# Hybrid decoder block: narrow split weights two to a buffer, the first weights of three projections asked for ahead, a last unit in halves

## The chip, the cores and the metric

The kernel runs on one core of a Trainium2 chip. The metric is device time in microseconds (us); lower is better. The engines are named as the profile names them: PE (matmuls) with PEld (its weight loads), DVE (vector), ACT (scalar), POOL (GpSimd) and SP, whose queue issues the transfers.

## The reference, cut to what matters

One decoder layer over 2048 positions of width 1024 in fp32. The change touches the feed-forward part and the last norm; what comes before them is the same in both kernels.

```python
def rmsnorm(x, g):
    y = x * lax.rsqrt(jnp.mean(x * x, axis=-1, keepdims=True) + NORM_EPS)
    return y * g
...
    x = x + mixed                       # mixers and output projection, unchanged here
    h2 = rmsnorm(x, norm2_g[l])
    ffn = (jax.nn.silu(h2 @ w_ffn_gate[l]) * (h2 @ w_ffn_up[l])) @ w_ffn_down[l]
    x = x + ffn
return rmsnorm(x, norm_f_g)
```

`D_MODEL` is 1024, `D_FF` 2816.

## The kernel before

Activations are kept transposed: 128 channels by 512 positions is a tile. The sequence is worked in two halves, and each half in two columns `j` of 512 positions. Every large product is a Strassen-like **unit** (`unit`, L385): a 2x2 block of weights times a 2x2 block of activations in seven products (`PRODUCTS`) instead of eight. An fp32 number is split into a high and a low part in fp32r (`split`, L151: ACT writes the high part at L153, DVE the low part at L154), and each product step is three matmuls, high x high, high x low, low x high (L381, L382, L383).

**Weights.** `raw_weights` loads four blocks of a unit into a tile `raw` (two buffers). `unit_weights` forms the sums of blocks on POOL (L364, L365, L366, L371) and splits seven quarters. Each quarter takes a tile `wq` of [128, 2, 512] from a pool of four buffers, whatever its width: 512 columns in the up projections, 384 in the later units of the down projection, 256 in its first four units (`wdown_first`).

**Feed-forward.** For each half, `ffn_up` runs 22 units over the operands `ops` (28 tiles of 512 KB, high and low parts); its results are split and stored to DRAM (`so`, then `sa`). `ffn_down` runs four groups of row blocks; group 0 has two blocks and four narrow units, the others three blocks and four units of 384 columns. In the first half the operands of `ffn_up` are made on the way; for the second half they lie in DRAM (`shB`, `shT`), and `load_h2` loads all 28 while `ffn_down(0)` ends. Each such load is placed after the load of the second-to-last weights (`raw_loads[-2]`).

**The last unit** (`last_unit`, L1019) multiplies without Strassen: four products of 18 matmuls over 512 positions, for two row blocks and two columns. To each belong a residual add (DVE, L1060), a square (ACT, L1062) and a gain (ACT, L1029). `norm(j)` sums the squares over partitions with a matrix of ones (PE, L1034 and L1035, fp32), takes Ln and Exp (ACT, L199, L200) and a Newton step (DVE, L201, L163 to L165), and copies the factor from PSUM to SBUF for POOL (ACT, L1037). `scale(j)` multiplies the eight tiles of a column by it, six on DVE and two on POOL (L1043), and stores each (SP, L148).

**Order.** A scheduler places the instructions on each engine from its own estimates, with the data dependences and some given orders (`tc.issue_after`). Each engine and SP's queue then works strictly in that order. The background work (splitting and storing the up projection's results, the next norm) is mixed in by `tick`.

Of the kernel before, what the change touches and what calls it, by code (L numbers as in the profile page):

```python
# [11 lines left out]
F32R = mybir.dt.float32r  # L12
U32 = mybir.dt.uint32
AF = mybir.ActivationFunctionType
ALU = mybir.AluOpType
# [36 lines left out]
def tile_hymba_block(ctx, tc, x, xt, win, wa, wgu, wout, wffn, wdown, wdown_first, small, out):  # L52
# [94 lines left out]
    def store(dst, src):  # L147
        return nc.sync.dma_start(dst, src)  # L148
# [92 lines left out]
    def no_operands():  # L241
        return {b: [] for _, b in PRODUCTS}
# [87 lines left out]
    def plain_unit(src, ops):  # L330
# [11 lines left out]
                us.append((r, j, settled(o, True), False))  # L342
        return us

    def weight_quarter(src):
        n = src.shape[-1]
        h = wqp.tile([P, 2, PB], F32R, name="wq", tag="wq")[:, :, 0:n]
        split(src, h[:, 0, :], h[:, 1, :])
        return h

    def raw_weights(src):
        n = src.shape[-1]
        raw = rawp.tile([P, 4 * PB], F32, name="raw", tag="raw")[:, 0 : 4 * n]
        raw = raw.rearrange("p (a n) -> p a n", a=4)
        raw_loads.append(load(raw, src))
        return raw

    def unit_weights(src):
        raw = raw_weights(src)
# [6 lines left out]
        pool.tensor_tensor(a11, s1, a11, ALU.subtract)  # L366
# [4 lines left out]
        pool.tensor_tensor(a12, a12, a11, ALU.subtract)  # L371
        w["S4"] = weight_quarter(a12)
        w["A22"] = weight_quarter(a22)
        return w

    def product_step(o, w, op, k, first):
        n = len(op)
        c = slice(k * P, (k + 1) * P)
        wh, wl = w[:, 0, c], w[:, 1, c]
        xh, xl = op[k][:, 0, :], op[k][:, 1, :]  # L380
        pe.matmul(o[:], wh, xh, start=first and k == 0, stop=False, skip_group_check=True)  # L381
        pe.matmul(o[:], wh, xl, start=False, stop=False, skip_group_check=True)  # L382
        return pe.matmul(o[:], wl, xh, start=False, stop=k == n - 1, skip_group_check=True)  # L383

    def unit(src, ops, into=None, onto=None):  # L385


        w = unit_weights(src)

        def mul(i, o=None):  # L390
            first = o is None
            o = bank() if first else o
            n, m = PRODUCTS[i]
            for k in range(len(ops[m])):
                product_step(o, w[n], ops[m], k, first)
            tick()
            return o

        def copied(name, o, at):
            if onto is not None:  # L400
                return plus(onto[at], o)
            t = tt(name) if into is None else into[at]
            act.activation(t[:], o[:], AF.Copy)  # L403
            return t

        def plus(t, o):
            dve.tensor_tensor(t[:], o[:], t[:], ALU.add)  # L407
# [499 lines left out]
    def ffn_up(half, ops):  # L907
        for m in range(NF // 2):
            us = unit(wffn[2 * m], ops)
# [12 lines left out]
            background.insert(0, split_later(s_act[half][m], values))  # L922
# [17 lines left out]
    def ffn_down(half):  # L940

        y, early = {}, {}

        def group_op(m, n):
            return early.pop((m, n)) if (m, n) in early else act_op(half, m, n)

        for u, m0 in enumerate(GROUPS):
# [10 lines left out]
            for d0 in range(0, KD, 2):  # L958
# [6 lines left out]
                if u == 0:  # L965
                    for d in (d0, d0 + 1):
                        if d < KD - 1:
                            pair = opp.tile([P, 2, PB], F32, name="y", tag="op")
                        for j in range(2):
                            y[d, j] = pair[:, j, :] if d < KD - 1 else bt("y")[:]  # L970
                    unit(src, ops, {(r, j): y[d0 + r, j] for r in range(2) for j in range(2)})
                    continue
                xs = []
                if u < 3:
# [44 lines left out]
    def last_unit(src, ops, b12, y, ssq):  # L1019


        raw = raw_weights(src)
        w = [weight_quarter(raw[:, i, :]) for i in (0, 1, 3, 2)]
        columns = (ops["B11"], ops["B21"]), (b12, ops["B22"])
        with tc.issue_after(last_hi[0].ins):
            act.preload_act_table_set("natural_log_exp_and_others")

        def gain(d, j):
            act.activation(y[d, j], y[d, j], AF.Copy, scale=col(C_GF + d))  # L1029

        def norm(j, q):

            tot, rb = bank("tot"), bank("rb")
            pe.matmul(tot[:], ones[:], ssq[j][:], start=True, stop=False)  # L1034
            pe.matmul(tot[:], ones[:], q[:], start=False, stop=True)  # L1035
            finish_rstd(ssq[j], tot, D, rb)
            act.activation(ssq[j][:], rb[:], AF.Copy)  # L1037
            return rb

        def scale(j, rb):  # L1040
            for d in range(KD):
                eng, by = (pool, ssq[j]) if d in (2, 5) else (dve, rb)
                eng.tensor_tensor(y[d, j], y[d, j], by[:], ALU.mult)  # L1043
                store(out[2 + j, :, d, :], y[d, j])

        for d in range(KD - 2):
            for j in range(2):
                gain(d, j)
        q, rbs = {}, []
        for j in range(2):  # L1050
            for r in range(2):
                o = bank()
                with ExitStack() as stack:
                    if j or r:
                        stack.enter_context(tc.issue_after(done.ins))
                    for i in range(2):
                        for k in range(len(b12)):
                            done = product_step(o, w[2 * r + i], columns[j][i], k, i == 0)
                yy = y[KD - 2 + r, j]
                dve.tensor_tensor(yy, o[:], yy, ALU.add)  # L1060
                q[j] = tt("q")
                act.activation(q[j][:], yy, AF.Square)  # L1062
                gain(KD - 2 + r, j)
                if not r:
                    pool.tensor_tensor(ssq[j][:], ssq[j][:], q[j][:], ALU.add)
                if j and not r:
                    rbs.append(norm(0, q[0]))
        rbs.append(norm(1, q[1]))
        for j in range(2):
            scale(j, rbs[j])  # L1070


    act.preload_act_table_set("natural_log_exp_and_others")
# [136 lines left out]
```

## Time and profile before

| | us |
|---|---|
| runs shown, median of 3 (lowest to highest) | 2093.23 (2089.54 to 2095.66) |
| profiled execution, device time | 2092.78 |
| its span, first to last instruction | 2090.8 |
| mean granted clock of PE in it | 0.993 |

The profiled execution lies 0.45 us under the median of the runs, and 2 us of its time lie outside the span. Where the profile gives a busy time, matmuls overlap: in the steady stretches about 22 of the 128x512 matmuls start in 5 us, though one is shown as 390 ns long. A lost stretch is best seen as matmuls missing from a window.

### The profile page before, as it was taken

Reading aid. Unit: us, or ns where it says so; the run is one execution under the profiler, and the core shown is the slowest. Engines: PE = TensorE matmul, PEld = TensorE weight load, DVE = VectorE, ACT = ScalarE, POOL = GpSimd, SP = SyncE. Lnnn points to the kernel's source line nnn. Section 1 sums busy time; section 2 is a strip of 40 time slices with the busy share of each in tenths; the row PEclk is TensorE's granted clock in tenths of the full one; section 3 lists DMA queues with packets and bytes.
Section 4 is the critical chain, followed back from the end, with each engine's and each line's share of the span. In section 5 each row is a group of like instructions: output and inputs, shape, how many; then the busy total and the mean of one; then the engine's idle time right before and its main releaser. Section 6 shows DMA issues by size and latency. Waiting matters only on the chain.

```text
span 2090.8 us, 26872 instructions
## 1 busy us (share of the span) xinstructions
PE 2029.0 (97%) x9133; PEld 1648.4 (79%) x9133; DVE 1434.0 (69%) x2049; ACT 970.1 (46%) x1921; POOL 876.7 (42%) x637
## 2 busy tenths in 40 slices
PE   5999999999999999999999999999999999999996
PEld 4778888887888887778788878887888888878884
DVE  6669786549754696787887566654776767666665
ACT  5555455656543345454555442223455444453234
POOL 3427222122102464555555434533655544434543
PEclk9999999999999999999999999999999999999998
DMA  7349485424586882654654587698454465488672
GB/s 275 126 152 307 154 338 162 146 96 145 181 306 212 329 286 93 230 224 174 227 222 171 214 326 280 235 358 349 146 206 158 169 228 191 164 349 307 267 272 111
DMA packets 189241, 464.43 MB, mean 222 GB/s; under 512 B 19824, under 2 KB 65072, under 8 KB 179504
## 3 DMA queue, kind: packets, MB, share of 16 engines
q1 hardware_dynamic: 189104, 462.72, 61.3%
q8 instruction: 72, 1.18, 0.2%
q14 instruction: 65, 0.53, 0.1%
HBM read 297.49 MB, written 165.15 MB: 221 GB/s over the span
## 4 chain that ended last, share of the span: by engine, by line
PE 77%; DVE 10%; DMA 6%; issue 3%; ACT 2%; POOL 2%; SPq 1%; DVEq 0%; ACTq 0%; POOLq 0%
PE mm L381 22%; PE mm L383 22%; PE mm L382 22%; DVE wq L154 2%; DVE h L510 2%; PE mm L814 2%; PE mm L815 2%; PE mm L817 2%; DMA op<-shT 1%; DVE so L154 1%; DVE op L154 1%; PE a_ps L578 1%; DMA shT<-so 1%; SPq L145 1%; PE o_ps L738 1%
## 5 line engine op out<-in xcount | busy, mean ns | idle before, releaser
L381 PE MATMUL mm<-op,wq 128*128 128x512 f32 x2499 | 979.6, 394 | 11.0 <-ACT wq L153 4.2
L382 PE MATMUL mm<-op,wq 128*128 128x512 f32 x2499 | 974.5, 390 | 0.0
L383 PE MATMUL mm<-op,wq 128*128 128x512 f32 x2499 | 962.4, 391 | 11.7 <-DVE wq L154 11.2
L154 DVE TENSOR_TENSOR wq<-raw,wq 128x512 fp32r<-128x512 f32 (+2 forms) x626 | 506.7, 815 | 243.2 <-ACT wq L153 241.4
L153 ACT ACTIVATE wq<-raw 128x512 fp32r<-128x512 f32 (+2 forms) x626 | 365.0, 588 | 600.5 <-PE mm L383 461.9
L381 PEld LDWEIGHTS mm<-op,wq 128*128 128x128 f32 x2499 | 469.9, 188 | 123.4 <-ACT wq L153 10.3
L383 PEld LDWEIGHTS mm<-op,wq 128*128 128x128 f32 x2499 | 469.8, 188 | 119.8 <-DVE wq L154 21.5
L382 PEld LDWEIGHTS mm<-op,wq 128*128 128x128 f32 x2499 | 470.1, 188 | 96.5 <-issue 1.0
L366 POOL TENSOR_TENSOR raw<-s,raw 128x512 f32<-128x512 f32 (+2 forms) x97 | 126.5, 1304 | 468.2 <-DVE wq L154 446.9
L364 POOL TENSOR_TENSOR s<-raw 128x512 f32<-128x512 f32 (+2 forms) x97 | 127.2, 1311 | 219.5 <-DMA raw<-in_wffn_dram 95.1
L407 DVE TENSOR_TENSOR y<-mm,y 128x512 f32<-128x512 f32 x185 | 127.4, 689 | 123.3 <-PE mm L383 122.6
L371 POOL TENSOR_TENSOR raw<-raw 128x512 f32<-128x512 f32 (+2 forms) x97 | 125.4, 1292 | 166.0 <-DVE wq L154 158.8
L407 DVE TENSOR_TENSOR c<-mm,c 128x512 f32<-128x512 f32 x198 | 135.6, 685 | 64.6 <-PE mm L383 63.3
L796 POOL TENSOR_TENSOR ssx<-ssx,q 128x512 f32<-128x512 f32 x52 | 76.2, 1479 | 160.7 <-ACT q L795 160.5
L365 POOL TENSOR_TENSOR raw<-raw 128x512 f32<-128x512 f32 (+2 forms) x97 | 136.5, 1407 | 4.9
L403 ACT ACTIVATE c<-mm 128x512 f32<-128x512 f32 x198 | 114.8, 586 | 16.2 <-PE mm L383 14.8
L154 DVE TENSOR_TENSOR so<-t,so 128x512 fp32r<-128x512 f32 x100 | 90.9, 914 | 27.3 <-ACT so L153 26.7
L153 ACT ACTIVATE wq<-s 128x512 fp32r<-128x512 f32 (+2 forms) x97 | 56.8, 585 | 96.2 <-PE mm L383 92.7
L814 PE MATMUL mm<-op,wq 128*128 128x512 f32 x256 | 100.9, 395 | 0.0
L815 PE MATMUL mm<-op,wq 128*128 128x512 f32 x256 | 99.8, 390 | 0.0
L154 DVE TENSOR_TENSOR wq<-s,wq 128x512 fp32r<-128x512 f32 (+2 forms) x97 | 79.7, 822 | 4.1 <-ACT wq L153 3.5
L153 ACT ACTIVATE so<-t 128x512 fp32r<-128x512 f32 x100 | 62.4, 626 | 42.1 <-DMA sa_B<-so 17.8
(178 smaller groups left out, 1849.8 us busy)
## 6 DMA issues: line engine op xcount, KB each, us to landing
raw<-in_wffn_dram SPq DMA_DIRECT2D x44, 1024.0 KB, 5.7
sa_T<-so SPq DMA_DIRECT2D x88, 512.0 KB, 4.9
op<-sa_T SPq DMA_DIRECT2D x88, 512.0 KB, 8.9
sa_B<-so SPq DMA_DIRECT2D x69, 512.0 KB, 3.5
op<-sa_B SPq DMA_DIRECT2D x69, 512.0 KB, 9.2
raw<-in_win_dram SPq DMA_DIRECT2D x23, 1024.0 KB, 5.6
raw<-in_wdown_dram SPq DMA_DIRECT2D x24, 768.0 KB, 5.9
sx<-y SPq DMA_DIRECT2D x48, 256.0 KB, 3.2
```

What stands on the lines that cost most here:

```text
L153: last_hi[:] = [act.activation(hi, src, AF.Copy)]
L154: return dve.tensor_tensor(lo, src, hi.bitcast(F32), ALU.subtract)
L364: pool.tensor_tensor(s1, a21, a22, ALU.add)
L365: pool.tensor_tensor(a21, a11, a21, ALU.subtract)
L366: pool.tensor_tensor(a11, s1, a11, ALU.subtract)
L371: pool.tensor_tensor(a12, a12, a11, ALU.subtract)
L381: pe.matmul(o[:], wh, xh, start=first and k == 0, stop=False, skip_group_check=True)
L382: pe.matmul(o[:], wh, xl, start=False, stop=False, skip_group_check=True)
L383: return pe.matmul(o[:], wl, xh, start=False, stop=k == n - 1, skip_group_check=True)
L407: dve.tensor_tensor(t[:], o[:], t[:], ALU.add)
L814: pe.matmul(o[e, j][:], wh, m[:, 0, :], start=k == 0, stop=False)
L815: pe.matmul(o[e, j][:], wh, m[:, 1, :], start=False, stop=False)
```

## The change

Line numbers of the new kernel are other ones: the matmuls L381 to L383 become L391 to L393, the adds of L407 L417, the copies of L403 L413, the residuals of the last unit L1067.

1. A quarter of at most 256 columns takes half of a `wq` buffer, so that two quarters share one. Units have seven quarters, so a pair can reach over two units.
2. `raw_weights` is called ahead of the operand loads for the first unit of `ffn_down(0)`, `ffn_up(1)` and `ffn_down(1)`. The loads of `load_h2` are placed after the last raw load (`raw_loads[-1]`), which is now the first one of `ffn_up(1)`.
3. In `last_unit` column 1 is worked in two halves of 256 positions, the order of PE and DVE is given by hand, the mean comes from a matrix of 1/1024 (so that the step L201 goes), the Newton step and the gain are folded into DVE's last multiplication, and POOL scales seven of the eight tiles of column 0 and two half tiles of column 1.

```diff
+    beside = []
+
     def weight_quarter(src):
         n = src.shape[-1]
-        h = wqp.tile([P, 2, PB], F32R, name="wq", tag="wq")[:, :, 0:n]
+        if n > PB // 2:
+            beside.clear()
+            h = wqp.tile([P, 2, PB], F32R, name="wq", tag="wq")[:, :, 0:n]
+        elif beside:
+            h = beside.pop()
+        else:
+            both = wqp.tile([P, 2, PB], F32R, name="wq", tag="wq")
+            beside.append(both[:, :, PB // 2 : PB // 2 + n])
+            h = both[:, :, 0:n]
         split(src, h[:, 0, :], h[:, 1, :])
...
     def load_h2():
-        ops, loads = no_operands(), raw_loads[-2]
+        ops, loads = no_operands(), raw_loads[-1]
...
     def ffn_down(half):
         y, early = {}, {}
+        raw = raw_weights(wdown_first[0])
...
-    for half in range(2):
-        ffn_up(half, load_h2() if half else h2)
-        ffn_down(half)
+    ffn_up(0, h2)
+    ffn_down(0)
+    raw = raw_weights(wffn[0])
+    ffn_up(1, load_h2(), raw)
+    ffn_down(1)
```

The last unit, new code only:

```python
known = bt("known", (P, P + KD))
means, gains = known[:, 0:P], known[:, P : P + KD]
dve.memset(means, 1.0 / D)
dve.tensor_scalar(gains, sml[:, C_GF : C_GF + KD], -0.5, None, ALU.mult)
...
def factor(j, tot, s, l, y0):
    rb = bank("rb")
    # three on DVE, in the given order: l = y0 * y0
    # l = (tot + EPS) * l ; rb = (l - 3) * y0
...
def scale(ds, j, s, rb):
    # on DVE: y = (y * gain) * rb, then a store of this part
...
def scale_beside(ds, j, s):
    # on POOL: y = y * ssq[j], then a store of this part
...
o = product(0, 0, whole)
q = residual(o, 0, 0, whole)
...
o = product(1, 0, whole)
q7 = residual(o, 1, 0, whole)
o = product(0, 1, sa)
p = residual(o, 0, 1, sa)
summed(tot[0], ssq[0], whole, first=True)
o = bank()
for n, _ in enumerate(steps(o, 1, 1, sa)):
    if n == 2:
        summed(tot[0], q7, whole, last=True)
l0 = logs(0, tot[0], whole)
p7 = residual(o, 1, 1, sa)
o = product(0, 1, sb)
summed(tot[1], ssq[1], sa, first=True)
rb0 = factor(0, tot[0], whole, *l0)
act.activation(ssq[0][:], rb0[:], AF.Copy)
scale_beside(range(KD - 1), 0, whole)
scale((KD - 1,), 0, whole, rb0)
r = residual(o, 0, 1, sb)
o = bank()
for n, _ in enumerate(steps(o, 1, 1, sb)):
    if n == 0:
        summed(tot[1], p7, sa, last=True)
l1 = logs(1, tot[1], sa)
summed(tot[2], ssq[1], sb, first=True)
summed(tot[2], r, sb)
rb1 = factor(1, tot[1], sa, *l1)
r7 = residual(o, 1, 1, sb)
scale((0, 1), 1, sa, rb1)
summed(tot[2], r7, sb, last=True)
l2 = logs(1, tot[2], sb)
scale((2, 3, 4, 5, 6, 7), 1, sa, rb1)
rb2 = factor(1, tot[2], sb, *l2)
act.activation(ssq[1][:, sb], rb2[:, sb], AF.Copy)
scale_beside((0, 1), 1, sb)
scale((2, 3, 4, 5, 6, 7), 1, sb, rb2)
```

On the engines the change moves instructions in three places. The first is ACT in `ffn_down(0)` between its second and third narrow unit. `wq` are the high parts of quarters, `y` copies of a finished product, `so` the background splits; `raw_11028` (before) and `raw_11021` (now) are the third unit's raw weights. Before:

```order
L403 ACTIVATE y_10928<-mm_10958 128x512
L153 ACTIVATE so_10984<-t2_10785 128x512
L403 ACTIVATE y_10929<-mm_10958 128x512
L153 ACTIVATE so_11003<-t3_10786 128x512
L153 ACTIVATE wq_11031<-raw_11028 128x256
L153 ACTIVATE wq_11037<-s1_11030 128x256
```

Now:

```order
L413 ACTIVATE y_10925<-mm_10951 128x512
L153 ACTIVATE wq_11024<-raw_11021 128x256
L153 ACTIVATE wq_11032<-raw_11021 128x256
L153 ACTIVATE wq_11024<-s1_11023 128x256
L413 ACTIVATE y_10926<-mm_10951 128x512
L153 ACTIVATE so_10977<-t2_10785 128x512
```

The third unit's first quarters have moved ahead of the copy `y` that waits for the second unit's last product. `ffn_down(1)` has the same move.

The second place is SP's queue ahead of `ffn_up(1)`. `shB11` are the first four operand tiles, `sx` and `y` belong to the norm of the first half. Before:

```order
L145 DMA op_12579<-shB11_0_412 128x1024
L148 DMA sx0_1_169<-y_10821 128x512
L148 DMA sx1_3_179<-y_10929 128x512
L148 DMA sx1_2_178<-y_10928 128x512
L148 DMA sx0_3_171<-y_10929 128x512
L145 DMA op_12581<-shB11_1_413 128x1024
L145 DMA y_12738<-sx0_1_169 128x512
L145 DMA y_12830<-sx0_2_170 128x512
L145 DMA op_12583<-shB11_2_414 128x1024
L145 DMA op_12585<-shB11_3_415 128x1024
L145 DMA y_12890<-sx0_3_171 128x512
L148 DMA sx0_4_172<-y_11026 128x512
```

Now:

```order
L145 DMA y_12876<-sx0_3_171 128x512
L148 DMA sx0_4_172<-y_11019 128x512
L145 DMA raw_12565<-in_wffn_dram 128x2048
L145 DMA op_12567<-shB11_0_412 128x1024
L145 DMA op_12569<-shB11_1_413 128x1024
L145 DMA op_12571<-shB11_2_414 128x1024
L145 DMA op_12573<-shB11_3_415 128x1024
L148 DMA sx1_4_180<-y_11019 128x512
L145 DMA op_12575<-shT1_0_416 128x1024
```

The raw load of `ffn_up(1)` stands behind the same store `sx0_4` as before (there it follows the last row shown); it is the four operand loads that have moved, from ahead of it to behind it. The first raw load of `ffn_down` has not moved in SP's queue: it has the same place in both programs, in both halves.

The third place is DVE at the end of the program. `rb` is a norm's factor in PSUM, `known` holds the gains. Before, the last rows:

```order
L1060 TENSOR_TENSOR y<-mm,y 128x512
L201 TENSOR_SCALAR ssx_17376<-tot 128x512
L163 TENSOR_TENSOR l<-y_17857 128x512
L164 SCALAR_TENSOR_TENSOR l<-l,ssx_17376 128x512
L165 SCALAR_TENSOR_TENSOR rb<-l,y_17857 128x512
L1043 TENSOR_TENSOR y<-y,rb 128x512 x6
```

Now:

```order
L1067 TENSOR_TENSOR y<-mm,y 128x256
L1104 SCALAR_TENSOR_TENSOR y<-y,known,rb 128x256 x8
L1084 TENSOR_TENSOR l<-y_17899 128x256
L1087 SCALAR_TENSOR_TENSOR l<-tot,l 128x256
L1093 SCALAR_TENSOR_TENSOR rb<-l,y_17899 128x256
L1104 SCALAR_TENSOR_TENSOR y<-y,known,rb 128x256 x6
```

The last residual now stands ahead of the multiplications of the half before it, and what follows the last norm is half as wide. PE's rows are the same in both programs up to the end of the last unit's second product.

More of the change, by code (lines that the diff above doesn't have):

```diff
@@ L379, in product_step, with unit @@
         wh, wl = w[:, 0, c], w[:, 1, c]
[L380 to L388, printed above, removed]
+        xh, xl = op[k][:, 0, s], op[k][:, 1, s]
+        pe.matmul(o[:, s], wh, xh, start=first and k == 0, stop=False, skip_group_check=True)
+        pe.matmul(o[:, s], wh, xl, start=False, stop=False, skip_group_check=True)
+        return pe.matmul(o[:, s], wl, xh, start=False, stop=k == n - 1, skip_group_check=True)
+    def unit(src, ops, into=None, raw=None, onto=None):
+        w = unit_weights(src, raw)
         def mul(i, o=None):
@@ L1040, in scale @@
[L1040 to L1044, printed above, removed]
-        for d in range(KD - 2):
[L1047 to L1067, printed above, removed]
@@ L1068, in last_unit, with queued @@
-        rbs.append(norm(1, q[1]))
-        for j in range(2):
-            scale(j, rbs[j])
+        known = bt("known", (P, P + KD))
+        means, gains = known[:, 0:P], known[:, P : P + KD]
+        dve.memset(means, 1.0 / D)
+        dve.tensor_scalar(gains, sml[:, C_GF : C_GF + KD], -0.5, None, ALU.mult)
+        halves = slice(0, PB // 2), slice(PB // 2, PB)
+        whole = slice(0, PB)
+        queues = {}
+        def queued(eng, issue):
+            with ExitStack() as stack:
+                if eng in queues:
+                    stack.enter_context(tc.issue_after(queues[eng].ins))
+                queues[eng] = issue()
@@ new lines, in steps, with product, residual @@
+        def steps(o, r, j, s):
+            for i in range(2):
+                for k in range(len(b12)):
+                    queued(pe, lambda: product_step(o, w[2 * r + i], columns[j][i], k, i == 0, s))
+                    yield
+        def product(r, j, s):
+            o = bank()
+            for _ in steps(o, r, j, s):
+                pass
+            return o
+        def residual(o, r, j, s):
+            yy = y[KD - 2 + r, j][:, s]
+            queued(dve, lambda: dve.tensor_tensor(yy, o[:, s], yy, ALU.add))
+            q = tt("q")
+            act.activation(q[:, s], yy, AF.Square)
+            return q
@@ new lines, in last_unit @@
+        for d in range(KD - 2):
+            act.activation(y[d, 0], y[d, 0], AF.Copy, scale=gains[:, d : d + 1])
+        for d in range(2):
+            yy = y[d, 1][:, halves[1]]
+            act.activation(yy, yy, AF.Copy, scale=gains[:, d : d + 1])
+        sa, sb = halves
+        tot = [bank("tot") for _ in range(3)]
+        o = product(0, 0, whole)
+        q = residual(o, 0, 0, whole)
+        act.activation(y[KD - 2, 0], y[KD - 2, 0], AF.Copy, scale=gains[:, KD - 2 : KD - 1])
+        pool.tensor_tensor(ssq[0][:], ssq[0][:], q[:], ALU.add)
```

55 lines of the change are left out of this document (41 added, 14 removed).

## The prediction

> **What bounds the kernel now.** I read the page first: busy shares, then the chain that ended last.
>
> ```profile
> PE 2029.0 (97%) x9133; PEld 1648.4 (79%) x9133; DVE 1434.0 (69%) x2049; ACT 970.1 (46%) x1921; POOL 876.7 (42%) x637
> PE 77%; DVE 10%; DMA 6%; issue 3%; ACT 2%; POOL 2%; SPq 1%; DVEq 0%; ACTq 0%; POOLq 0%
> ```
>
> PE is busy nearly throughout, and the change takes no product away. It can only win back stretches in which PE starves, and the tail. So next come PE's waits, in windows around the two starts of the down projection (the first is shown, the second lists the same two), the start of the second up projection, and the end:
>
> ```profile
> PE mm L381 <- ACT wq L153: 1.5, 1, 1.5
> PE mm L381 <- DVE y L407: 0.8, 1, 0.8
> ...
> PE mm L381 <- ACT c L403: 1.7, 1, 1.7
> PE mm L381 <- DMA op<-shT: 0.4, 1, 0.4
> ...
> PE tot L1035 <- ACT q L1062: 4.5, 1, 4.5
> ```
>
> These waits are short. Since matmuls overlap, I count matmuls in windows of 5 us (columns: stretch, length, busy time and count on PE, PEld, DVE, ACT, POOL, clock, DMA share, GB/s):
>
> ```profile
> 1200.00:1205.00 5.00, 5.00 (x24) 4.14 (x23) 3.67 (x6) 3.21 (x7) 0.00 (x0) 1.00 1.02 410
> 1230.00:1235.00 5.00, 2.71 (x11) 1.50 (x9) 2.11 (x5) 1.95 (x5) 1.27 (x2) 1.00 0.43 175
> 1870.00:1875.00 5.00, 3.08 (x11) 1.93 (x12) 2.69 (x6) 2.25 (x5) 0.97 (x2) 1.00 0.33 134
> 1455.00:1460.00 5.00, 3.31 (x14) 2.36 (x13) 2.86 (x3) 2.81 (x6) 2.50 (x2) 1.00 0.23 66
> ```
>
> A full window counts 23 or 24. Twelve matmuls are missing at 1230 and at 1870, nine at 1455: 12 x 0.227 = 2.7 us, twice, and 2.0 us. (0.227 us is the pitch of a 128x512 matmul, from the tail's rows below.) These three places and the tail are what the change can touch.
>
> **Starts of the down projection.** The timeline there:
>
> ```profile
> 1206.93 0.42 ACT L153 ACTIVATE wq<-s 128x256 fp32r<-128x256 f32 x1 [1.88 <-PE mm L383]
> 1219.84 0.33 SPq L145 DMA_DIRECT2D raw<-in_wdown_first_dram  x1
> 1231.36 0.50 PE L381 MATMUL mm<-op,wq 128*128 128x512 f32 x1 [0.78 <-DVE y L407]
> 1233.05 0.60 ACT L403 ACTIVATE y<-mm 128x512 f32<-128x512 f32 x1 [4.64 <-PE mm L383]
> 1234.07 0.41 ACT L153 ACTIVATE wq<-raw 128x256 fp32r<-128x256 f32 x1
> 1234.52 0.50 PE L381 MATMUL mm<-op,wq 128*128 128x512 f32 x1 [1.51 <-ACT wq L153]
> ```
>
> ACT's splits wait for PE to free a `wq` buffer (1206.93). The third unit's first quarter, on which PE stops until 1234.52, is split only at 1234.07, because in ACT's order it stands behind the copy of 1233.05, which waits for PE itself. With two quarters to a buffer the splits run ahead: in the new order the quarter stands before that copy, its buffer is free by then, and its raw load stands two stores earlier in SP's queue than the one issued at 1219.84. I expect the 1.51 us to go, with the slow restart behind it and short stalls nearby: 2.4 us of the 2.7 plus what is scattered. The 0.78 us stays: two products add into one bank with the same add on DVE between them. Bounds: 0 each if another wait takes its place, 3.4 if the first stall goes too. Two starts: **-4.8 us** (0 to -6.8).
>
> Nothing comes of loading the first weights ahead at these two places: in the program these loads keep their place in SP's queue. The pairing adds no instruction; a buffer is held longer, until both quarters are used, and twice the room covers that.
>
> **Start of the second up projection.** SP's queue, the DMA share there, and a piece of the chain:
>
> ```profile
> 1401.64 0.85 SPq L145 DMA_DIRECT2D op<-shB  x2
> 1405.50 0.36 SPq L145 DMA_DIRECT2D raw<-in_wffn_dram  x1
> 1444.42 0.32 SPq L145 DMA_DIRECT2D op<-shT  x1
> ...
> 1444.42 10.24 DMA op<-shT
> ...
> 1389.00:1392.00 3.00, 3.00 (x15) 2.49 (x14) 1.88 (x4) 0.53 (x1) 1.52 (x2) 1.00 0.23 87
> 1413.00:1416.00 3.00, 3.00 (x15) 2.49 (x14) 2.95 (x4) 0.53 (x1) 2.51 (x3) 1.00 0.85 298
> 1416.00:1419.00 3.00, 3.00 (x15) 2.49 (x14) 1.18 (x2) 0.53 (x1) 1.12 (x1) 1.00 1.02 409
> 1449.00:1452.00 3.00, 3.00 (x15) 2.44 (x14) 0.40 (x1) 0.63 (x1) 0.67 (x1) 1.00 1.02 425
> ```
>
> From 1416 to 1452 the DMA engines are full: 28 operand tiles of 512 KB and raw weights. The last tile is issued at 1444.42, lands 10.24 us later, at 1454.66, and PE waits for it (the 0.4 us above). This chain runs through transfers, so what is queued ahead of it delays PE. Before, the first four tiles, 2.1 MB, went out ahead of the raw weights, the last two of them at 1401.64. Now all four stand behind the raw load, which stays behind a store that waits for DVE, at 1405.50. Those 2.1 MB at 410 GB/s are 5.1 us of transfer that move into the full stretch. Not all is felt: before, I estimate about 1 MB issued just ahead of 1405.50 as still in flight, and 15% of 3 us are free at 1413. I take half: the last tile lands 2.6 us later, and PE with it. The four tiles themselves are needed only some 28 us before the last one (126 matmuls earlier in PE's order x 0.227), at about 1426, so they are in time. Bounds: 0 and +5.1. **+2.6 us.**
>
> **The last unit.** Tail rows, and the issues of the output:
>
> ```profile
> 2060.76 0.69 DVE L1060 TENSOR_TENSOR y<-mm,y 128x512 f32<-128x512 f32 x1 [2.47 <-PE mm L383]
> 2064.64 1.02 PE L1034 MATMUL tot<-ssx,ones 128*128 128x512 f32 x2
> 2064.83 0.69 DVE L1060 TENSOR_TENSOR y<-mm,y 128x512 f32<-128x512 f32 x1 [3.39 <-PE mm L383]
> 2071.03 3.68 DVE L1043 TENSOR_TENSOR y<-y,rb 128x512 f32<-128x512 f32 x6 [0.66 <-ACT ssx L1037]
> 2071.07 2.49 POOL L1043 TENSOR_TENSOR y<-y,ssx 128x512 f32<-128x512 f32 x2 [3.51 <-ACT ssx L1037]
> 2074.63 0.68 DVE L1060 TENSOR_TENSOR y<-mm,y 128x512 f32<-128x512 f32 x1
> 2078.14 0.69 ACT L199 ACTIVATE l<-tot,eps 128x512 f32<-128x512 f32 x1 [1.41 <-PE tot L1035]
> ...
> L148 SPq DMA_DIRECT2D out_dram<-y x16: 332/406/593, 2071.7 to 2086.9; - x16
> ...
> DMA to landing us min/median/max: 2.0/2.7/3.0
> ```
>
> Before, the last residual (2074.63) stands behind six multiplications of column 0, and the whole second norm follows. A product of 18 matmuls takes 2064.83 - 2060.76 = 4.07 us, 0.227 us each. Prices of what is new, from the nearest rows:
>
> ```profile
> 651.29 0.39 PE L740 MATMUL o_ps<-carry,kq 128*128 128x128 f32 x2
> 651.73 0.39 PE L740 MATMUL o_ps<-carry,kq 128*128 128x128 f32 x2
> L153 ACT ACTIVATE wq<-raw 128x256 fp32r<-128x256 f32 x48 | 19.0, 413 | 25.0 <-PE mm L383 16.6 <-POOL raw L366 5.7 <-POOL raw L371 1.9
> L154 DVE TENSOR_TENSOR wq<-s,wq 128x256 fp32r<-128x256 f32 x8 | 3.6, 445 | 0.0
> L510 DVE SCALAR_TENSOR_TENSOR h<-h,sml,rb x16: 740/1402/1787, 708.2 to 744.4; 128x512 f32<-128x512 f32 x16
> L269 POOL TENSOR_TENSOR t<-h x12: 1296/1675/2495, 142.0 to 1067.1; 128x512 f32<-128x512 f32 x12
> ```
>
> No fp32r matmul of 256 columns is in the trace. Four narrow fp32 ones with their weight loads start in 0.44 us, 0.11 each; the wide one takes 0.227. I take 0.12, since half the columns of the wide one is 0.114 and the weight load fits into 0.11. [...]
>
> Now from 2060.76, where both programs stand alike. First half product 2.2, sum matmul 0.85, half of the next product 1.1, second sum 1.0: sums ready at 2065.9. Ln and Exp 0.69 + 0.64, three DVE steps of 0.72, the copy 0.6: POOL starts column 0 at 2070.0. Its seven tiles at 1.25 end at 2078.8, then two halves at some 0.75 at 2080.3. DVE meanwhile does the first half's norm (1.3), the last residual, eight half multiplications (8 x 0.39), the last norm's three steps and six more, and ends near 2079.7, before POOL. In SP's order five stores follow POOL's last one: 5 x 0.41, last issue at 2082.0. Before, from the last issue (2086.9) to the span's end (2090.8) were 3.9 us behind a full queue; with 3.4 now, the end is at 2085.4: -5.4.
>
> Against that: DVE's norm steps with both inputs in SBUF now run beside POOL. The rows of L510 show such a meeting, 0.74 to 1.79 us with `rb` in SBUF. Four such steps of 0.42 hold POOL up by up to 1.7 us. With all of it the end is at 2087.1 or, with DVE's own delays, 2088.0: -2.8. I take the middle: **-4.1 us**. If half products cost as much as whole ones, everything comes some 4 us later: about 2090, -0.8.
>
> **Sum.** -4.8 + 2.6 - 4.1 = -6.3 us on the profiled execution's 2092.78 us: **2086.5 us**, 0.32% under the median of the runs (2093.23), which lies 0.45 above that execution. About 0.3% (6.3 us, 2086.95) is what a measurement of this kernel can tell from no change, so the forecast lies on that bound.
>
> **The rivals.**
>
> *The operand loads are not felt* (18%). The backlog of 1405 and the gap at 1413 swallow the four tiles. For it: the share of 0.23 at 1389 shows that the queue is not full throughout; against it: 36 us at 1.02 behind it. 2092.78 - 4.8 - 4.1 = 2083.9.
>
> *The narrow pairs don't do what they say* (16%): the third unit's raw weights still come late through a full queue (1.02 at 1200), or ACT stops at another copy; only the scattered bits go. Also under it: half products at the price of whole ones. For it: the wait is one of order on ACT, not of room alone. 2092.78 - 0.5 + 2.6 - 4.1 = 2090.8.
>
> *All lost matmuls come back* (9%): 3.4 at each start and no delay at the second up projection, 2092.78 - 6.8 - 4.8 = 2081.2.
>
> *POOL becomes the bound at the end, and the kernel slower* (7%). Seven wide tiles stand on POOL where there were two. L269 shows one at 2.50 us, twice the 1.25 beside DVE operations that read a factor from PSUM. At 2.4 us the seven end at 2086.8, two halves at 2089.4, and five stores and the last landing bring the end to 2094.5: +3.7 in place of -4.1, 2094.3 in all. It decides from about 2.2 us a tile, where the tail's loss eats the 2.2 us gained elsewhere. Against it: DVE's multiplications there read `rb` from PSUM, as in the rows of 2071. [...]
>
> **Chances and range.** The forecast holds 50%, with its own range of 2083 to 2090, a little more than half of it under 2086.95. Faster: 0.27 of it, 0.17 of the unfelt loads, 0.09 of the full gain: 0.53. Slower by over 0.3% (2099.5) needs POOL's case with a full 5.1 us in the loads: 0.06. Same: 0.41. Range for 8 in 10: 2080.5 to 2091.5.
>
> **What would show it.** Right: the windows near 1230 and 1870 count 20 or more matmuls, the wait for ACT `wq` there is gone and that for DVE `y` stays; at the second up projection PE's wait for `op<-shT` grows to about 3 us and SP issues `shB` behind the raw weights; in the tail POOL's seven at 1.25 to 1.5 us each end last, and the span ends 15 to 18 us after its first one starts. Wrong: a `wq` or `raw` wait of over 1 us at the down starts, the last `shT` landing as early as before, half matmuls over 0.15 us apart, or an end set by DVE or SP rather than POOL.

## The result and the profile after

| | median us (lowest to highest), runs | ratio to before, 95% interval |
|---|---|---|
| before | 2090.44 (2086.77 to 2095.66), 10 | |
| changed | 2084.24 (2078.83 to 2087.08), 10 | 0.9968 [0.9956, 0.9981] |

The medians lie 6.2 us apart. By the ratio the changed kernel is 0.32% faster, with an interval of 0.19 to 0.44%. Its profiled execution took 2085.32 us, with a span of 2083.6 and a mean granted clock of 0.995. The page after, busy shares and the chain that ended last:

```profile
PE 2026.7 (97%) x9175; PEld 1651.2 (79%) x9175; DVE 1429.0 (69%) x2057; ACT 965.2 (46%) x1918; POOL 882.6 (42%) x642
PE 79%; DVE 6%; DMA 3%; issue 2%; POOL 1%; ACT 1%; SPq 0%; DVEq 0%; POOLq 0%; ACTq 0%
```

DVE and DMA have lost 4 and 3 points of the chain; the bound is still PE. PE's waits after, at the first start of the down projection (two rows) and at the second up projection (two rows):

```profile
PE mm L391 <- DVE y L417: 0.8, 1, 0.8
PE mm L393 <- DVE wq L154: 0.3, 1, 0.3
...
PE mm L391 <- ACT wq L153: 2.0, 1, 2.0
PE mm L391 <- ACT c L413: 1.7, 1, 1.7
```

At the down projection the 1.5 us for ACT `wq` are gone and the 0.8 for DVE `y` stands, as forecast. ACT's rows there show why:

```profile
1225.80 0.71 ACT L153 ACTIVATE wq<-raw 128x256 fp32r<-128x256 f32 x2
1230.46 0.60 ACT L413 ACTIVATE y<-mm 128x512 f32<-128x512 f32 x1 [3.64 <-PE mm L393]
```

The third unit's first quarters are split at 1225.80, 4.7 us ahead of the copy that waits for PE; before, the first of them came 1.0 us behind it. At the up projection the 0.4 for `op<-shT` has not grown; it has vanished, and 2.0 us for ACT `wq` stand there instead. The windows of the same places, and the stretch where that new wait lies:

```profile
1225.00:1230.00 5.00, 4.22 (x19) 3.19 (x18) 2.66 (x5) 1.52 (x5) 1.75 (x3) 1.00 0.51 207
1865.00:1870.00 5.00, 4.22 (x19) 3.20 (x18) 2.14 (x5) 2.04 (x5) 1.77 (x3) 1.00 0.82 337
1430.00:1435.00 5.00, 3.12 (x14) 2.25 (x12) 1.39 (x2) 2.24 (x4) 2.55 (x2) 1.00 1.02 412
1435.00:1440.00 5.00, 4.92 (x14) 3.61 (x15) 0.69 (x1) 0.03 (x1) 1.29 (x1) 0.67 1.02 411
1450.00:1455.00 5.00, 3.65 (x16) 2.55 (x14) 4.09 (x4) 3.21 (x6) 2.89 (x2) 1.00 0.16 62
```

11 matmuls have become 19 at the two down starts. At the up projection a window with 14 is followed by another one with 14, in which the granted clock is 0.67: PE is busy there and only slower.

A window depends on where its edges fall. So for sizes I use the start times of single matmuls. PE's order is not quite the same in all these kernels, though I wrote so above: of some 8400 matmuls of the units about 440 stand at other places in the changed program, in groups in both down projections and at the second up start. At each mark of the table the same matmuls lie behind it and the same one starts, so that the marks can be compared. Time between them, in us, with the kernels of the experiments below that carry one part alone:

| from matmul to matmul | before | changed | pairs alone | halves alone | loads ahead alone |
|---|---|---|---|---|---|
| 200 to 5300, unchanged code | 1107.27 | 1104.96 | 1104.94 | 1105.25 | 1105.50 |
| 5300 to 5600, first down start | 71.91 | 69.69 | 69.72 | 73.48 | 71.99 |
| 6200 to 6460, second up start | 62.59 | 65.00 | 63.42 | 62.82 | 65.12 |
| 6460 to 6550, behind it | 20.54 | 20.53 | 21.94 | 20.53 | 21.89 |
| 8050 to 8350, second down start | 72.24 | 69.67 | 69.71 | 72.18 | 74.02 |
| 8350 to 9000, rest of that projection | 148.78 | 149.33 | 149.32 | 148.25 | 148.00 |
| 9000 to the span's end, last unit | 50.77 | 46.70 | 51.22 | 46.55 | 50.77 |

The first row shows how far two executions differ where nothing was changed: 2.3 us. The row of 6460 to 6550 and the odd 73.48 and 74.02 hold dips of the clock, of which more below.

The last unit after, from the timeline:

```profile
2057.46 0.28 PE L391 MATMUL mm<-op,wq 128*128 128x256 f32 x1
...
2057.66 0.69 DVE L1067 TENSOR_TENSOR y<-mm,y 128x512 f32<-128x512 f32 x1 [2.47 <-PE mm L393]
...
2059.49 0.28 PE L393 MATMUL mm<-op,wq 128*128 128x256 f32 x1
...
2066.93 10.74 POOL L1111 TENSOR_TENSOR y<-y,ssx 128x512 f32<-128x512 f32 x9 [5.42 <-ACT ssx L1141]
...
2075.63 2.44 DVE L1104 SCALAR_TENSOR_TENSOR y<-y,known,rb 128x256 f32<-128x256 f32 x6 [0.45 <-ACT ssx L1159]
...
2074.03 6.84 SPq L148 DMA_DIRECT2D out_dram<-y  x14
```

The residual at 2057.66 is the one at 2060.76 before, so 3.1 us are to be added for a comparison with the forecast. The 18 matmuls of the first half product start between 2057.46 and 2059.49, (2059.49 - 2057.46) / 17 = 0.12 us apart. POOL's nine multiplications end at 2077.67 and DVE's last six at 2078.07. But SP issues its last 14 stores back to back, 6.84 / 14 = 0.49 us each, until 2080.87. Neither POOL nor DVE sets the end; SP's queue does.

### The profile page after: what moved, and what is told of

It reads as the page before. It is cut to its first block, busy times and chain, and to the rows that moved or that the text cites. A ratio compares the mean times of both kernels' runs of the same rounds, so it can differ in the third digit from the quotient of the medians.

```text
span 2083.6 us, 26960 instructions
## 1 busy us (share of the span) xinstructions
PE 2026.7 (97%) x9175; PEld 1651.2 (79%) x9175; DVE 1429.0 (69%) x2057; ACT 965.2 (46%) x1918; POOL 882.6 (42%) x642
## 4 chain that ended last, share of the span: by engine, by line
PE 79%; DVE 6%; DMA 3%; issue 2%; POOL 1%; ACT 1%; SPq 0%; DVEq 0%; POOLq 0%; ACTq 0%
PE mm L391 23%; PE mm L393 23%; PE mm L392 22%; PE mm L824 3%; PE mm L825 2%; PE mm L827 2%; DVE wq L154 2%; DVE so L154 1%; DMA raw<-in_wffn_dram 1%; DMA shT<-so 1%; PE o_ps L748 1%; PE o_ps L750 1%; DMA op<-sa_T 1%; PE sc L724 0%; POOL t L927 0%
## 5 line engine op out<-in xcount | busy, mean ns | idle before, releaser
L391 PE MATMUL mm<-op,wq 128*128 128x512 f32 x2511 | 982.1, 393 | 10.8 <-ACT c L413 5.0
L393 PE MATMUL mm<-op,wq 128*128 128x512 f32 x2511 | 964.8, 390 | 10.4 <-DVE wq L154 10.2
L391 PEld LDWEIGHTS mm<-op,wq 128*128 128x128 f32 x2511 | 472.4, 188 | 122.7 <-ACT c L413 8.6
L393 PEld LDWEIGHTS mm<-op,wq 128*128 128x128 f32 x2511 | 472.5, 188 | 116.7 <-DVE wq L154 18.8
L417 DVE TENSOR_TENSOR y<-mm,y 128x512 f32<-128x512 f32 x185 | 127.2, 689 | 131.5 <-PE mm L393 131.2
L381 POOL TENSOR_TENSOR raw<-raw 128x512 f32<-128x512 f32 (+2 forms) x97 | 124.9, 1288 | 164.7 <-DVE wq L154 157.6
L417 DVE TENSOR_TENSOR c<-mm,c 128x512 f32<-128x512 f32 x198 | 135.3, 683 | 64.9 <-PE mm L393 63.6
L413 ACT ACTIVATE c<-mm 128x512 f32<-128x512 f32 x198 | 114.9, 587 | 17.3 <-PE mm L393 15.8
```

Of the source, the lines that this page charges most:

```text
L391: pe.matmul(o[:, s], wh, xh, start=first and k == 0, stop=False, skip_group_check=True)
L393: return pe.matmul(o[:, s], wl, xh, start=False, stop=k == n - 1, skip_group_check=True)
```

## The experiments

Every ratio is against the kernel before, run on the same chip in the same session.

### Each part alone

Pairs alone: the kernel before with part 1 of the change.

```diff
+        elif beside:
+            h = beside.pop()
+        else:
+            both = wqp.tile([P, 2, PB], F32R, name="wq", tag="wq")
+            beside.append(both[:, :, PB // 2 : PB // 2 + n])
```

> The kernel before with the narrow pairs alone. By the recorded steps: -4.8 us, a ratio near 0.9977; at both starts of the down projection PE's wait of 1.5 us for ACT wq is gone, the one of 0.8 for DVE y stays, the lag to the kernel before grows by about 2.4 us at each; the second up projection and the last unit stay as before (the wait for op<-shT 0.4 us, 30 us from the last unit's first residual to the span's end). Rival, that the changed kernel's gain at these two places needs the loads ahead: the wait of 1.5 us is still there, ratio 1.000.

Measured: 0.9977 [0.9967, 0.9988], 2085.92 us against 2091.36. Both down starts shorten to 69.7 us, by 2.2 and 2.5, and the wait for ACT `wq` is gone without any load ahead. Two things were not expected. The second up start is 0.8 us longer and followed by a dip, and the rest of the second down projection takes 0.5 us more here; over the ten traces with pairs it takes 149.1 to 149.9 us, over the three without 148.0 to 148.8, so about 1.1 us of the gain is given back. PE waits 0.4 us for `op<-sa_T` and 0.3 for DVE `wq` there in the changed kernel, against 0.6 for DVE `wq` before, which explains little of it; the rest was not followed.

Halves alone: the kernel before with part 3.

```diff
+        o = product(0, 1, sa)
+        p = residual(o, 0, 1, sa)
...
+        scale_beside(range(KD - 1), 0, whole)
```

> The kernel before with the last unit in halves alone. By the recorded sum: -4.1 us, a ratio near 0.998; from the last unit's first residual to the span's end 25.9 us instead of 30.0; half matmuls 0.12 us apart. Which of POOL and SP ends it: if POOL, SP's stores wait for POOL at the end; if SP, its last 20 stores are issued back to back some 0.49 us apart, and the last issue lies over 2 us behind POOL's and DVE's last multiplication. Rival: the half products pay only where the pairs came first, 0 us.

Measured: 0.9973 [0.9963, 0.9984], 2086.51 us. The last unit takes 46.55 us instead of 50.77, 4.2 less, and it is SP that ends it, as in the changed kernel: the last issue lies 2.4 us behind DVE's last multiplication. The down starts keep their wait of 1.5 us; the halves do not need the pairs.

Loads ahead alone: the kernel before with part 2.

```diff
-        ops, loads = no_operands(), raw_loads[-2]
+        ops, loads = no_operands(), raw_loads[-1]
...
+    raw = raw_weights(wffn[0])
+    ffn_up(1, load_h2(), raw)
```

> The kernel before with the first weights loaded ahead alone, at all three places. Recorded: 0 at the two starts of the down projection, +2.6 us at the second up projection, a ratio near 1.0012; by the recorded way PE waits about 3 us for op<-shT there. Second theory (ACT's order): the same +2 to +3 us, but as a wait of about 2.0 us for ACT wq, with a dip of the granted clock behind it perhaps, and no wait for op<-shT. Rival: the loads do pay at the down projection, and its windows near 1230 and 1870 count 15 or more instead of 11.

Measured: 1.0014 [1.0005, 1.0022], 2093.86 us against 2091.36: slower. PE's waits at the second up start:

```profile
PE mm L381 <- ACT wq L153: 2.0, 1, 2.0
PE mm L381 <- ACT c L403: 1.7, 1, 1.7
PE mm L381 <- DMA op<-shT: 1.5, 1, 1.5
```

Both theories' waits are there at once. The first down start takes 71.99 us, as before (71.91), so the loads ahead bring nothing there. The second one holds a dip of the clock (74.02).

### The changed kernel without the loads ahead

```diff
-        ops, loads = no_operands(), raw_loads[-1]
+        ops, loads = no_operands(), raw_loads[-2]
...
-    raw = raw_weights(wffn[0])
-    ffn_up(1, load_h2(), raw)
+    ffn_up(1, load_h2())
```

Of the two edits only the first matters: with `raw_loads[-2]` alone the instructions of all engines stand in the same order as without any load ahead.

> The changed kernel without the loads ahead (narrow pairs and the last unit in halves stay). By the recorded sum 2.6 us under the changed kernel: -8.9 us against before, a ratio near 0.9957, and from the stretch 1430 to 1470 the wait of 2.0 us for ACT wq is gone. Rival, that the changed kernel lost there by a dip of the granted clock that comes by chance (1.7 us of it): 1 us under the changed kernel, ratio 0.9965, and the dip can be in this kernel's profile too.

Measured: 0.9944 [0.9931, 0.9958], 2079.14 us, the fastest of the study. The stretch from 6200 to 6460 takes 62.63 us, as before, and PE waits 0.5 us for `op<-shT` there and not at all for ACT `wq`. A second time, beside the kernel with fewer stores:

> The kernel without the loads ahead again, beside the one with fewer stores and on another chip or hour than the first time: ratio 0.9944 to 0.996; the stretch from matmul 6200 to 6550 83.2 us, with no wait for ACT wq, and no dip of the granted clock where PE waits under 1 us for op<-shT.

Measured: 0.9957 [0.9942, 0.9971], 2082.21 us. This time PE waited 1.0 us for `op<-shT`, and a dip followed, so that 6200 to 6550 took 86.4 us and not 83.2.

### Transfers or ACT's order

The change moves three things at the second up start. On SP, four `shB` loads go behind the raw weights. On ACT, the second unit's first quarter goes behind the silu copy L452, which waits for PE by way of DVE. On PE, the first four matmuls with that quarter go ahead of three of the first unit, so that PE asks for the quarter 0.7 us sooner. I had seen only the first. ACT's rows there, from the timeline before and then, with PE's, after:

```profile
1437.59 0.63 ACT L153 ACTIVATE wq<-raw 128x512 fp32r<-128x512 f32 x1 [1.60 <-PE mm L383]
1438.32 0.63 ACT L442 ACTIVATE c<-c 128x512 f32<-128x512 f32 x1
```

```profile
1433.88 0.63 ACT L452 ACTIVATE c<-c 128x512 f32<-128x512 f32 x1 [2.33 <-DVE c L417]
1434.42 0.61 ACT L153 ACTIVATE wq<-raw 128x512 fp32r<-128x512 f32 x1
1435.08 0.50 PE L391 MATMUL mm<-op,wq 128*128 128x512 f32 x1 [1.96 <-ACT wq L153]
```

Before, the split starts as PE frees its buffer, and the silu copy follows. After, the copy is first: DVE's sum for it starts at 1433.16, as PE ends a product, and the split that could have run then runs at 1434.42. Three kernels tell the transfers from ACT's order. First, the changed kernel again on the same chip:

> The changed kernel again, beside the next three on the same chip. Ratio 0.996 to 0.998. In its profile the stretch from matmul 6200 to matmul 6550 (the start of the second up projection) takes 83.8 to 85.6 us (85.5 in the first profile, 83.1 in the kernel before, 83.2 without the loads ahead), the wider figure where a dip of the granted clock falls into it. PE's wait of 2.0 us for ACT wq is there each time; if the dip is chance, it can be missing, and then a wait of about 1 us for op<-shT stands there.

Measured: 0.9974 [0.9963, 0.9986], 2083.40 us; 6200 to 6460 in 65.16 us, the wait of 2.0 us there, a dip behind it.

Then the changed kernel with the quarter put ahead of the silu copy again:

```diff
+            nxt = raw_weights(wffn[1])
+            first = weight_quarter(nxt[:, 0, :])
+            with tc.issue_after(last_hi[0].ins):
+                sg = {(r, j): silu(c, p) for r, j, c, p in us}
```

> The changed kernel, with ACT's split of the second unit's first quarter put ahead of the silu copy again; SP's order stays the changed one (four shB tiles behind the raw weights). If the transfers set the price (the recorded way): the wait of 2.0 us for ACT wq is gone, PE waits 2.5 to 3 us for op<-shT instead, the stretch from matmul 6200 to 6550 still takes 84.8 to 85.7 us, ratio as the changed kernel's within 0.0005. If ACT's order sets it: no such wait, the stretch takes 83.2 us, 2.3 us under the changed kernel, ratio lower by 0.0011.

Measured: 0.9982 [0.9973, 0.9991], 2085.60 us. PE's waits:

```profile
PE mm L391 <- DMA op<-shT: 2.2, 1, 2.2
PE mm L391 <- ACT c L413: 1.7, 1, 1.7
PE mm L393 <- DVE wq L154: 1.1, 1, 1.1
PE mm L391 <- ACT wq L153: 0.7, 1, 0.7
```

The wait for ACT is down from 2.0 to 0.7; what is left is PE's earlier use of the quarter. But 1.1 us for DVE's low part of the same quarter stand beside it, so that the stall at this place is still 1.8 us:

```profile
1431.79 1.28 POOL L375 TENSOR_TENSOR raw<-raw 128x512 f32<-128x512 f32 x1
1431.81 1.80 DVE L154 TENSOR_TENSOR wq<-raw,wq 128x512 fp32r<-128x512 f32 x1
```

Beside a POOL row that began 0.02 us ahead of it, DVE's row took 1.80 us; before, the same row (at 1438.25), with no POOL row beside it, takes 0.69. So this kernel hardly shortens the stall and decides less than it was built for. 6200 to 6460 takes 65.77 us (65.16 in the changed kernel beside it), with a wait of 2.2 us for `op<-shT`. A dip followed; with it 6200 to 6550 took 88.6 us, outside the range written for either theory.

Last, ACT's order of the changed kernel on the SP order of before:

```diff
+                if n == 0:
+                    held = last_silu[0] if half == 1 and m == 0 else None
...
+                stack.enter_context(tc.issue_after(held.ins))
             w = {"A11": weight_quarter(a11)}
```

> The kernel without the loads ahead (pairs and halves stay), with ACT's order of the changed kernel at that place: the silu copy ahead of the split; SP's order is that of before. If the transfers set the price: PE stops about 2 us for ACT wq, then no longer waits for op<-shT (0.6 us of it saved), the stretch from matmul 6200 to 6550 takes 84.5 us (83.2 without the flip), and 1.7 us more with a dip of the clock. If ACT's order is the whole cause: 85.3 to 85.5 us, as the changed kernel, ratio 0.0011 over that without the loads ahead (0.9944 then).

Measured: 0.9965 [0.9954, 0.9976], 2082.22 us; 6200 to 6460 in 63.5 us, to 6550 in 84.05: 0.9 over the kernel without the loads ahead (83.17), under the 84.5 written for the transfers and far from 85.3. PE waited 1.3 us for ACT `wq` and not the 2 that were written, as PE's order there is not the changed one, and 0.8 for `op<-shT` behind it in any case. ACT's order alone is worth up to 0.9 us, and perhaps nothing: the other kernels with pairs and SP's order of before take 62.6 to 63.7 us to matmul 6460.

The rows of SP's queue and the landing of its last operand tile decide it. The last `shT` load is issued, before and after:

```profile
1444.42 0.32 SPq L145 DMA_DIRECT2D op<-shT  x1
```

```profile
1442.24 0.32 SPq L145 DMA_DIRECT2D op<-shT  x1
```

Matmul 6200 starts at 1394.78 and 1390.34, so the issue comes 49.6 us behind it before and 51.9 after, 2.3 later. In the other traces with the changed SP order it is 51.9 to 52.4 us, in those with the order of before 49.7 to 50.7. The tile lands 62.3 to 63.0 us behind matmul 6200 in the five traces with the changed order and 59.9 to 61.0 in the eight others, whatever PE waited for ahead of it. In all 13 matmul 6457, the first that reads it, starts 0.04 to 0.10 us behind the landing. So the transfers set the length of this stretch.

### The end of the program

Six of the last half stores from ACT's queue:

```diff
-        scale((2, 3, 4, 5, 6, 7), 1, sb, rb2)
+        scale((2, 3, 4, 5, 6, 7), 1, sb, rb2, nc.scalar)
```

> The changed kernel, with the last six half stores (the second half of column 1, DVE's) issued from ACT's queue instead of SP's. If SP's issues set the end: SP's 18 stores end near POOL's last multiplication, ACT's six go out as DVE finishes, and the span ends some 2.4 us earlier (from the last unit's first residual to the end 23.5 instead of 25.9 us), ratio lower by 0.0011. If POOL sets it, as recorded: the last store still goes out 0.4 us behind POOL's last multiplication and the end is earlier by less than 0.5 us.

Measured: 0.9972 [0.9961, 0.9982], 2083.44 us; from matmul 9000 to the end 45.83 us instead of 46.71 in the changed kernel beside it: 0.9 us, between the two expectations. The issues of the two queues:

```profile
2077.23 2.44 DVE L1104 SCALAR_TENSOR_TENSOR y<-y,known,rb 128x256 f32<-128x256 f32 x6 [0.45 <-ACT ssx L1159]
2077.74 3.89 ACTq L1106 DMA_DIRECT2D out_dram<-y  x6
2078.11 1.96 SPq L148 DMA_DIRECT2D out_dram<-y  x3
```

SP did set the end, but side by side the two queues need 0.65 us for each issue instead of 0.49, so that DVE's last result (2079.67) still waits for its issue until ACT's queue ends at 2081.63.

Fewer stores: tiles 2 to 5 of column 1 once at full width, on the kernel without the loads ahead.

```diff
+                if d in held:
+                    if s != halves[1]:
+                        continue
+                    store(out[2 + j, :, d, whole], y[d, j][:, whole])
```

> The kernel without the loads ahead (pairs and halves stay), and of column 1 the tiles 2 to 5 stored once at full width instead of in two halves: 20 stores of the last unit instead of 24, the same bytes. If the number of SP's issues sets the end (0.49 us each, back to back): 4 x 0.49 = 2.0 us less queue, bounded by DVE's last multiplication, so 1.5 to 2.0 us: from matmul 9000 to the span's end 44.7 to 45.2 instead of 46.7, ratio 0.9936 (0.9944 without it). If the bytes set it, or POOL as recorded: within 0.4 us of 46.7.

Measured: 0.9954 [0.9939, 0.9969], 2080.89 us; from matmul 9000 to the end 46.69 us: nothing. The four stores left out were issued early, where SP now has gaps (13 stores in 7.68 us at the end, against 14 in 6.84). What counts is the burst of eight stores behind the last norm, of which four now carry twice the bytes. The last one is issued 2.05 us behind DVE's last result instead of 2.41, but lands 2.3 us later and not 1.8.

The parts that paid, together: pairs and halves without the loads ahead, five of the last stores from ACT's queue.

> Narrow pairs and the last unit in halves, without the loads ahead, and five of the last half stores (tiles 3 to 7 of column 1, second half) issued from ACT's queue. From the runs so far: 0.9944 and 0.9957 without the loads ahead, less 0.9 us as ACT's queue gave on the changed kernel (45.8 instead of 46.7 us from matmul 9000 to the span's end): a ratio of 0.994 to 0.9955, under both kernels. Rival, that the two queues slow each other's issues as much as they share: 46.5 us and no gain over 0.9944 to 0.9957.

Measured: 0.9965 [0.9953, 0.9978], 2083.64 us against 2090.19. The last unit took 45.84 us, as hoped, but at the second up start PE waited 1.5 us for `op<-shT` even so, and a dip followed. It is faster than the kernel before; better than the changed kernel it has not been shown to be, nor better than pairs and halves alone. Taken over all comparisons, the five of kernels with pairs and halves and without the loads ahead gave 0.9944 to 0.9965, the four of kernels with them 0.9968 to 0.9982. The means, 0.9957 and 0.9974, lie 0.0017 or 3.6 us apart. Of the five only silu first ran beside kernels with the loads ahead, with 0.9965 against 0.9972 to 0.9982.

## Why the prediction was right, point by point

**The result.** Forecast: 6.3 us off the profiled execution, 2086.5 us. Measured: 6.2 us between the medians, at 2084.24. The 2.3 us between forecast and median are the base: before stood at 2090.44 this time and not at 2092.78. The two profiled executions lie 7.5 us apart, 2.3 of them in code that was not changed.

**Starts of the down projection, -4.8.** Measured 2.2 and 2.6 us in the changed kernel, -4.8 in all, by the mechanism given: the quarter moved ahead of a copy that waits for PE. PE's own order at the narrow units changed too; what of the gain hangs on that was not tried apart. The loads ahead do nothing there, as written. Not in the sum: the 1.1 us given back later in the second down projection. The windows count 19, one short of what was named.

**Start of the second up projection, +2.6.** Measured +2.4 (65.00 against 62.59 us to matmul 6460), +2.5 with the loads ahead alone and +2.6 in the repeated run. The step as put was right: counted from matmul 6200 the last operand tile lands 2.4 us later (62.31 against 59.88), where 2.6 was written, and PE's matmul 6457 starts with it (62.41 against 59.93). What the step had wrong is how it shows. I had looked at SP's order only and not at ACT's and PE's, so I named a wait for `op<-shT` of 3 us as the mark. In the changed kernel PE stalls earlier, on ACT's split and a slower clock (0.67 from 1435 to 1440), and reaches the last tile as it lands. One hides the other: with the loads alone and with ACT's stores no dip followed the first stall, 1.5 us for `op<-shT` came out, and the stretch to matmul 6460 was as long (65.12 and 65.07).

**The last unit, -4.1.** Measured -4.07 (46.70 against 50.77), and -4.2 with the halves alone. Half matmuls: 0.12 us taken, 0.12 measured. POOL's start: forecast 2070.0, measured 2066.93 + 3.1 = 2070.0. The step that failed is "POOL sets the end". POOL's nine multiplications took 10.74 us against 10.3 forecast; seven wide ones 1.37 each on average and not 1.25:

```profile
L1111 POOL TENSOR_TENSOR y<-y,ssx 128x512 f32<-128x512 f32 x7 | 9.4, 1372 | 5.4 <-ACT ssx L1141 5.4
L1093 DVE SCALAR_TENSOR_TENSOR rb<-l,y 128x256 f32<-128x256 f32 x2 | 1.8, 924 | 0.1
L1087 DVE SCALAR_TENSOR_TENSOR l<-tot,l 128x256 f32<-128x256 f32 x2 | 0.8, 424 | 0.1
```

I had priced a store at 0.41 us of SP, its issue alone, and let five of them follow POOL. In the trace each takes 0.49, and 24 of them make a queue that ends 3.2 us behind POOL. The bounds on that end (2085.4 to 2088.0) held it, at 2083.6 + 3.1 = 2086.7. That -4.1 came out all the same is in part luck: the 1.3 us that I had added to 2085.4 for the meeting of DVE and POOL were filled by SP's queue, whose last store goes out 1.6 us later than the 2082.0 written. The meeting of DVE and POOL came as the old row of L510 had it: the half norm step with both inputs in SBUF (L1093) took 0.92 us beside POOL, the one with an input from PSUM (L1087) 0.42. On POOL's side it was small: the four wide multiplications that met a step with both inputs in SBUF (L1084 or L1093) took 1.44 to 1.45 us, the other three 1.26 to 1.29, which makes 0.7 us where up to 1.7 was allowed for.

**The rivals.** Loads not felt: excluded, loads ahead alone are slower (1.0014 [1.0005, 1.0022]). Narrow pairs do nothing: excluded (0.9977 [0.9967, 0.9988]). All lost matmuls back: no, the 0.8 us for DVE `y` stays at both starts and the second up start lost 2.4; its sum also takes 4.8 us for the last unit, where 4.1 gives 2081.9. POOL the bound: excluded, it ends 3.2 us ahead of SP's last issue.

**Chance in the agreement.** Unchanged code differs by 2.3 us between the two first profiles, and a dip of the clock is worth 1.4 to 2.7 us; the single terms are better known than the sum of any two executions.

## What to carry to other kernels

Where a load is moved, read the order of every engine around it and not of SP's queue alone: a scheduler that places one load elsewhere can also turn round a split and a copy on ACT, and matmuls on PE. Two waits in a row on different things hide each other (6200 to 6460 took 65.00 us with 2.0 for ACT `wq`, a dip and no wait for `op<-shT`, and 65.12 with the 2.0, no dip and 1.5 for `op<-shT`), so a stall named in a profile is worth only what is left when the next one comes up; take one away and look at the sum. Price a burst of small stores at the queue's pitch (0.49 us here) and not at the length of one issue (0.41), and compare long stretches between the same two instructions when two executions differ by chance as much as the change is worth (here 2.3 us in unchanged code).

## What the runs showed of the hardware

**The granted clock falls at short waits.** The records of the clock show pieces of 3.4 or 6.8 us at half speed in mid-kernel; in the changed kernel's trace one of 3.4 us at 0.50 begins at 1436.7. At the second up start two waits of PE follow each other within 5 us: one for `op<-shT` and one of 1.7 us for ACT `c`. In the five traces in which the first was 0.4 to 0.8 us (before, halves alone, fewer stores, the first run without the loads ahead, silu first) no dip followed. In the six in which it was 1.0 to 2.2 us, a dip followed each time. From one without the loads ahead, then one whose clock fell:

```profile
PE mm L391 <- ACT c L413: 1.7, 1, 1.7
PE mm L391 <- DMA op<-shT: 0.5, 1, 0.5
```

```profile
PE mm L391 <- ACT c L413: 1.7, 1, 1.7
PE mm L391 <- DMA op<-shT: 1.0, 1, 1.0
...
1450.00:1455.00 5.00, 5.00 (x12) 3.94 (x13) 2.96 (x4) 1.51 (x3) 1.28 (x1) 0.50 0.68 248
```

Twelve matmuls start in 5 us there instead of 22 to 24. From matmul 6460 to 6550 this makes 21.9 to 23.3 us instead of 20.5. So half a microsecond more of waiting can cost 1.4 to 2.7 us more. This is probably why the loads ahead cost 3.6 us over all comparisons, and only 2.4 in a trace without a dip at that place; it was not tried apart.

The 13 traces taken together show more. Within one trace all dips start whole multiples of 3.413 us apart, to within 0.01 us (before, at 36.00, 66.72 and 152.05: 9 and 25 times 3.413): they lie on a grid, which lies elsewhere in each execution. Cut by this grid, the stretches from 200 to 2050 us give some 7000 cells of 3.413 us at full clock. By PE's rows, whose ends are modelled, PE was idle for 1.77 us or more in 11 of these cells, and a dip began right behind each of the 11 (in the changed kernel's trace, 1.80 us in the cell that begins at 1433.3). In 14 cells it was idle for 1.5 to 1.77 us, and a dip began behind 3 (before, none behind the 1.76 us in the cell that begins at 1230.7). In all the others it was idle for less, and no dip began. In these traces, then, the dips went with PE's idle time summed within one cell of 3.413 us: none under 1.5 us, always from 1.77 us on. Where a wait fell on the grid differed from one execution to the next. The single wait of 2.0 us for ACT `wq` drew a dip in two of four traces; in the other two the grid cut it, and no cell held more than 1.53 us of it. The two dips cost nothing, as PE then reached the last tile as it landed (0.10 us behind the landing in the changed kernel). No single wait at these places was longer than 2.2 us.

**Two queues are not two times one.** Stores issued back to back from SP alone took 0.49 us each, from SP and ACT at once 0.65 on average. The second queue saved 0.9 us of the 2.4 by which the last issue started behind DVE's last result.
